# Gate matmuls on the residual stream, and 32-row matmuls padded to 128 rows, in a two-layer recurrent decoder step

## The chip, the cores and the metric

The kernel runs on one core of a Trainium2 chip. The metric is device time in microseconds (us): the median of three runs is 2811.98 us, from 2808.73 to 2813.22. The engines are named as in the profile: PE (TensorE matmuls), PEld (its weight loads), DVE (VectorE), ACT (ScalarE), POOL (GpSimd) and SP (SyncE). POOL computes little here. It mostly issues DMAs.

## The reference

A trunk of two layers runs over 256 prompt tokens and 8 samples of 4 tokens each, 288 columns in all. Layer 0 mixes with a diagonal state-space model and gated linear attention, layer 1 with an mLSTM of 4 heads. Each layer is followed by a squared-ReLU MLP. The change concerns layer 1, cut here to what matters:

```python
xn = rmsnorm(h, W['norm_mix'][layer])
proj = xn @ W['w_in_odd'][o]            # q, k, v, output gate, then 8 columns: ig, fg
ig = proj[..., 4*ML_WIDTH : 4*ML_WIDTH + ML_HEADS] + b_i
fg = proj[..., 4*ML_WIDTH + ML_HEADS :] + b_f
# per head: fcum, dmat, m come from ig and log_sigmoid(fg)
w  = exp(dmat - m[..., None])
sc = (q @ k.T) * w
num = sc @ v + wp[..., None] * (q @ cm)        # cm: 512 x 512 memory of the head
den = sum(sc, -1) + wp * (q @ nm)
h   = num / maximum(abs(den), exp(-m))[..., None]
c_new = decay * cm + sum_s wk * k_s v_s        # written out for all 8 samples
```

Every sample has its own 512 x 512 memory per head. All of these memories are read from HBM, updated and written back (64 pieces of 512 KB in and 64 out).

## The kernel before, in words

The residual stream lives in SBUF as `h` (tile `hr`), 16 blocks of 128 features by 288 columns, in f32. Every large product takes three matmuls in a reduced format: the weight is split into `wh` (ACT, L187) and `wl` (DVE, L188), the activation into `xh` and `xl`, where `xh` is `h` times the norm weight, rounded, and `xl` the rest. `mm` (L202 to L204) issues the three products per 128 x 128 block of weight. Weights come in pieces of 512 x 256 (`raw`, by SP). There are four buffers each of `raw`, `wh` and `wl`, and a cast waits until PE has finished with the buffer that it overwrites. So casts run one to two pieces ahead of PE, no more.

`run` goes through the list of pieces. After each it gives every side generator a turn (`pump`). So matmuls, casts and side work are interleaved in one fixed order per engine, settled when the program is built, and each engine works through its list strictly in that order. The side generators here are `ml_gates` (once, at the start of layer 1), `ml_head` (one per head), and `ml_mem`.

`ml_gates` multiplies the 8 gate columns of the weight (tile `wg`, zero-padded to 32 columns) with `xh` and then with `xl`: 32 plain f32 matmuls, four at a time on the four 32-column strips of the array (L1289). Its loads (L1272 to L1280) are on POOL.

`ml_head(h)` builds the weights `w`: 128 x 416 with the prompt's three blocks in columns 0 to 383 and the samples' block in columns 384 to 415, where only 32 partitions are used. DVE adds the masks (L1418 to L1420), ACT takes exponentials (L1421 to L1424), PE computes the scores (L1429), DVE multiplies (L1431, L1432). Later PE sums `w` for the denominators (L1482 to L1485) and multiplies it with the values `vt1` for the numerators (L1500 to L1502). The samples' parts, L1484 and L1502, contract over 32 partitions, all others over 128. L1484 runs once per head, L1502 four times. `w` has one buffer.

`ml_mem` walks through the 64 memory pieces. For each, PE makes an update, DVE applies it to the tile `cin` (L1563), POOL stores the tile (L1565), and then POOL loads the piece that is six ahead into the same buffer (L1533). That load waits until the store has landed. While it waits, POOL does nothing else.

Of the kernel before, what the change touches and what calls it, by code (L numbers as in the profile page):

```python
# [7 lines left out]
F32 = mybir.dt.float32  # L8
# [3 lines left out]
ALU = mybir.AluOpType  # L12
# [3 lines left out]
T = 288  # L16
TP = 256
NS = 32
D = 2048
ND = D // 128  # L20
# [1225 lines left out]
class Layer1:  # L1246
    def ml_open(self):
        self.mlc = ExitStack()
        pool = lambda n, b=1: self.mlc.enter_context(self.tc.tile_pool(name=n, bufs=b))
        p = self.mlp1 = pool("ml")  # L1250
        pool_d = self.mlc.enter_context(self.tc.tile_pool(name="mld", bufs=1, space=DRAM))
        self.q1 = p.tile([128, 4, T], F32, name="q1")
        self.k1 = p.tile([128, 4, T], F32, name="k1")
        self.vt1 = p.tile([128, 3, 512], F32, name="vt1")
        self.kw1 = p.tile([128, 3, 512], F32, name="kw1")
        self.hn, self.so, self.smp = {}, {}, {}
        self.yy = {}
        self.rb4 = p.tile([4, 608], F32, name="rb4")
        self.aT = p.tile([128, 3, 4], F32, name="aT")
        self.wkT = p.tile([128, 3, 4], F32, name="wkT")  # L1260
        self.dec = p.tile([128, 4], F32, name="dec")
        self.rb_dram = pool_d.tile([4, 608], F32, name="rb_dram")
        self.n0T = p.tile([128, 4, 32], F32, name="n0T")
        self.rbk = p.tile([128, T], F32, name="rbk")

    def ml_gates(self):
        nc, I, O = self.nc, self.I, self.O
        v, act = nc.vector, nc.scalar
        pc = self.tc.tile_pool(name="mlg", bufs=1, side="right")
        p = pc.__enter__()  # L1270
        wg = p.tile([128, ND, 32], F32, name="wg")
# [7 lines left out]
        n0 = p.tile([32, 512], F32, name="n0r")  # L1279
        nc.gpsimd.dma_start(out=n0, in_=I["state_mlstm_n"][0].rearrange("b h d -> (b h) d"))  # L1280
        yield
        yield
        v.tensor_scalar(out=self.rbk, in0=self.rbc, scalar1=512.0 ** -0.5, scalar2=None, op0=ALU.mult)
        ps = self.pss.tile([128, T], F32, name="s")
        for i in range(4):
            for x in (self.xh, self.xl):
                for c in range(4):
                    k = 4 * i + c
                    nc.tensor.matmul(ps[32 * c:32 * c + 32, :], lhsT=wg[:, k, :], rhs=x[:, k, :].bitcast(F32),  # L1289
                                     start=i == 0 and x is self.xh, stop=i == 3 and x is self.xl)  # L1290
        gs = p.tile([128, T], F32, name="gs")
        v.tensor_mul(out=gs, in0=ps, in1=self.rbc)
        yield
# [105 lines left out]
    def ml_head(self, h):  # L1399
        nc, I, O = self.nc, self.I, self.O  # L1400
        v, act = nc.vector, nc.scalar
        q, k, vt, kw = self.q1, self.k1, self.vt1, self.kw1
        yield from self.until("gates")
        p = self.mlh
# [10 lines left out]
        yield  # L1415

        w = p.tile([128, 416], F32, name="w")
        v.tensor_add(out=w[:, 0:128], in0=bb[:, 0:128], in1=self.c("tri"))  # L1418
        v.tensor_add(out=w[:, 256:384], in0=bb[:, 128:256], in1=self.c("tri"))
        v.tensor_add(out=w[0:32, 384:416], in0=bb[0:32, TP:T], in1=self.c("tri_s")[0:32])  # L1420
# [5 lines left out]
        ps = self.pss.tile([128, 416], F32, name="s")  # L1426
        for s0, n, t0, t1, o in ((0, 128, 0, 256, 0), (128, 128, 128, 256, 256), (256, 32, 256, 288, 384)):
            for d in range(4):
                nc.tensor.matmul(ps[0:n, o:o + t1 - t0], lhsT=k[:, d, s0:s0 + n], rhs=q[:, d, t0:t1],  # L1429
                                 start=d == 0, stop=d == 3)  # L1430
# [4 lines left out]
        for i, n in enumerate((128, 128, 32)):  # L1435
            ps = self.pss.tile([128, 4, 128], F32, name="s")
            for d in range(4):
# [9 lines left out]
                        op=ALU.mult)  # L1447
        qn = p.tile([128, 4, NS], F32, name="qn")
        v.tensor_tensor(out=qn.rearrange("p d (b s) -> p d b s", s=4), in0=qp.rearrange("p d (b s) -> p d b s", s=4),
                        in1=self.n0T[:, :, h:32:4].rearrange("p d (b o) -> p d b o", o=1).to_broadcast([128, 4, 8, 4]),  # L1450
                        op=ALU.mult)
# [10 lines left out]
        ps = self.pss.tile([128, 128], F32, name="s")  # L1462
        for i, (n, c) in enumerate(((128, "selp"), (128, "selp"), (32, "sels"))):
            for d in range(4):
                nc.tensor.matmul(ps[32 * d:32 * d + 32, :], lhsT=self.c(c)[0:n], rhs=kw[0:n, i, d * 128:d * 128 + 128],  # L1465
                                 start=i == 0, stop=i == 2)
# [13 lines left out]
        ps = self.pss.tile([128, T], F32, name="s")  # L1480
        on = self.ones
        nc.tensor.matmul(ps[:, 0:256], lhsT=on, rhs=w[:, 0:256], start=True, stop=False)  # L1482
        nc.tensor.matmul(ps[:, 128:256], lhsT=on, rhs=w[:, 256:384], start=False, stop=True)
        nc.tensor.matmul(ps[:, TP:T], lhsT=on[0:32], rhs=w[0:32, 384:416], start=True, stop=False)  # L1484
        nc.tensor.matmul(ps[:, TP:T], lhsT=on, rhs=qn[:, 0, :], start=False, stop=True)  # L1485
        rec = s["rec"] = p.tile([128, T], F32, name="rec", bufs=2)
        act.activation(out=rec, in_=ps, func=AF.Abs)
# [9 lines left out]
        for e in range(4):  # L1497
            es = slice(e * 128, e * 128 + 128)
            ps = self.pss.tile([128, T], F32, name="s")
            nc.tensor.matmul(ps[:, 0:256], lhsT=vt[:, 0, es], rhs=w[:, 0:256], start=True, stop=False)  # L1500
            nc.tensor.matmul(ps[:, 128:256], lhsT=vt[:, 1, es], rhs=w[:, 256:384], start=False, stop=True)  # L1501
            nc.tensor.matmul(ps[:, TP:T], lhsT=vt[0:32, 2, es], rhs=w[0:32, 384:416], start=True, stop=True)  # L1502
            v.tensor_mul(out=hn[:, e, :], in0=ps, in1=rec)
            yield

        for d in range(4):
            ds = slice(d * 128, d * 128 + 128)
            ps = self.pss.tile([128, 512], F32, name="s")
# [371 lines left out]
```

## Time and profile before

| what | value |
|---|---|
| runs, median (lowest to highest) | 2811.98 us (2808.73 to 2813.22) |
| profiled execution | 2810.88 us, span 2809.1 us |
| mean granted TensorE clock | 0.996 |
| PE busy | 2780.6 us (99%) |
| DVE, ACT, POOL busy | 62%, 48%, 8% |
| HBM traffic over the span | 181 GB/s |

PE has work in flight for nearly the whole span, and the chain of work that ended last is made of PE's pieces. The layer-1 mixer lies between about 1300 and 1910 us. There the DMA engines carry the memory pieces beside the weights: they are busy 67% to 82% of the time, against 55% in the MLP between 500 and 1300 us.

Times of single instructions in a timeline are start, duration, engine, line, what is written from what, and in brackets the idle time before it and what ended it. A plain f32 matmul shows as two records of PE.

### The profile page before, as it was taken

How to read it: one execution, taken by the hardware profiler on the slowest of the kernel's cores; microseconds unless marked ns; L12 is line 12 of the kernel's file. 1: busy time of each engine (PE TensorE's matmuls, PEld its weight loads, DVE VectorE, ACT ScalarE, POOL GpSimd, SP SyncE). 2: the span in 40 equal slices, each digit the busy share in tenths (PEclk: the TensorE clock that was granted, in tenths of full speed). 3: DMA queues.
4: the chain of work that ended last, by engine and by line, in shares of the span. 5: the costliest groups of instructions: out<-in, count | busy, mean ns of one | idle time of the engine just before them, and what ended most of it. 6: DMA issues, size and time to landing. Idle time of an engine off the chain costs nothing.

```text
span 2809.1 us, 52656 instructions
## 1 busy us (share of the span) xinstructions
PE 2780.6 (99%) x20680; PEld 2692.6 (96%) x20680; DVE 1728.4 (62%) x3259; ACT 1344.2 (48%) x2460; POOL 212.3 (8%) x326
## 2 busy tenths in 40 slices
PE   9999999999999999999999999999999999999999
PEld 8988999999999999999988898889999999999999
DVE  7887668555555555556566665867655555555555
ACT  5646755544444444445433343445544444444445
POOL 3110112000000000000112222210000000000000
PEclk9999999999999999999999999999999999999999
DMA  7454567555555555555677878875555555555554
GB/s 218 123 160 136 160 198 227 159 171 166 165 163 166 162 168 164 165 165 145 198 230 240 279 241 269 271 254 173 164 167 162 169 165 165 160 170 160 169 165 136
DMA packets 449656, 511.87 MB, mean 182 GB/s; under 512 B 23298, under 2 KB 423324, under 8 KB 449376
## 3 DMA queue, kind: packets, MB, share of 16 engines
q1 hardware_dynamic: 414320, 412.67, 48.7%
q0 software_dynamic: 28096, 90.16, 10.1%
q10 hardware_dynamic: 6992, 5.68, 0.6%
q8 instruction: 163, 2.67, 0.4%
q14 instruction: 85, 0.70, 0.1%
HBM read 460.08 MB, written 47.56 MB: 181 GB/s over the span
## 4 chain that ended last, share of the span: by engine, by line
PE 52%; ACT 0%; DVE 0%; issue 0%; DVEq 0%
PE g L202 16%; PE g L203 15%; PE g L204 15%; PE s L1561 1%; PE n L1555 1%; PE s L1510 1%; PE s L1429 0%; PE s L1500 0%; PE s L1438 0%; PE s L1502 0%; PE s L1465 0%; PE s L1501 0%; PE s L1587 0%; PE s L1382 0%; ACT wh L187 0%
## 5 line engine op out<-in xcount | busy, mean ns | idle before, releaser
L187 ACT ACTIVATE wh<-raw 128x512 fp32r<-128x512 f32 x1556 | 962.5, 629 | 1199.0 <-PE g L203 1151.7
L188 DVE TENSOR_TENSOR wl<-raw,wh 128x512 fp32r<-128x512 f32 x1556 | 1036.5, 689 | 662.8 <-ACT wh L187 651.0
L202 PE MATMUL g<-xh,wh 128*128 128x288 f32 x3856 | 1157.5, 300 | 3.0 <-DVE gy L948 1.4
L204 PE MATMUL g<-xh,wl 128*128 128x288 f32 x3856 | 1137.2, 295 | 3.4 <-DVE wl L188 3.4
L203 PE MATMUL g<-xl,wh 128*128 128x288 f32 x3856 | 1140.0, 296 | 0.0
L202 PEld LDWEIGHTS g<-xh,wh 128*128 128x128 f32 x3856 | 725.3, 188 | 14.4 <-issue 9.5
L204 PEld LDWEIGHTS g<-xh,wl 128*128 128x128 f32 x3856 | 728.0, 189 | 5.0 <-DVE wl L188 4.9
L203 PEld LDWEIGHTS g<-xl,wh 128*128 128x128 f32 x3856 | 726.3, 188 | 5.2 <-issue 3.3
L203 PE MATMUL g<-hl,wh 128*128 128x288 f32 x2048 | 606.2, 296 | 0.0
L204 PE MATMUL g<-hh,wl 128*128 128x288 f32 x2048 | 605.2, 296 | 0.0
L202 PE MATMUL g<-hh,wh 128*128 128x288 f32 x2048 | 604.7, 295 | 0.0
L202 PEld LDWEIGHTS g<-hh,wh 128*128 128x128 f32 x2048 | 389.1, 190 | 0.0
L204 PEld LDWEIGHTS g<-hh,wl 128*128 128x128 f32 x2048 | 384.0, 188 | 0.0
L203 PEld LDWEIGHTS g<-hl,wh 128*128 128x128 f32 x2048 | 383.7, 187 | 0.0
L1737 DVE TENSOR_TENSOR hr<-hr,g 128x288 f32<-128x288 f32 x256 | 116.4, 455 | 186.5 <-PE g L204 186.5
L1729 ACT ACTIVATE us<-sq 128x288 f32<-128x288 f32 x128 | 56.9, 445 | 146.3 <-DVE sq L1728 146.3
L1728 DVE SCALAR_TENSOR_TENSOR sq<-g,rbc 128x288 f32<-128x288 f32 x128 | 58.5, 458 | 94.5 <-PE g L204 94.3
L1563 DVE SCALAR_TENSOR_TENSOR cin<-cin,wps,s 128x512 f32<-128x512 f32 x128 | 89.7, 743 | 7.2 <-PE s L1561 6.5
L1533 POOL DMA_DIRECT2D cin<-in_state_mlstm_c_dram x64 | 45.3, 708 | 316.3 <-DMA out_sample_mlstm_c_dram<-cin 293.8
L1344 POOL DMA_DIRECT2D out_sample_mlstm_m_dram<-mo x1 | 0.6, 615 | 838.7 <-DVE mk L1348 838.7
L1730 ACT ACTIVATE hh<-us 128x288 fp32r<-128x288 f32 x128 | 57.0, 445 | 4.1
L203 PE MATMUL g<-yl,wh 128*128 128x288 f32 x192 | 56.7, 295 | 0.0
(506 smaller groups left out, 1939.7 us busy)
## 6 DMA issues: line engine op xcount, KB each, us to landing
raw<-in_w_mlp_up_dram SPq DMA_DIRECT2D x256, 512.0 KB, 3.7
raw<-in_w_mlp_down_dram SPq DMA_DIRECT2D x256, 512.0 KB, 3.7
raw<-in_w_in_odd_dram SPq DMA_DIRECT2D x128, 512.0 KB, 4.8
raw<-in_w_in_even_dram SPq DMA_DIRECT2D x64, 512.0 KB, 4.1
cin<-in_state_mlstm_c_dram POOLq DMA_DIRECT2D x64, 512.0 KB, 5.2
out_sample_mlstm_c_dram<-cin POOLq DMA_DIRECT2D x64, 512.0 KB, 5.7
raw<-in_w_out_even_dram SPq DMA_DIRECT2D x32, 512.0 KB, 4.6
raw<-in_w_out_odd_dram SPq DMA_DIRECT2D x32, 512.0 KB, 3.6
```

The source lines that it names most:

```text
L187: nc.scalar.activation(out=wh[:, 0:n], in_=src, func=AF.Copy)
L188: nc.vector.tensor_tensor(out=wl[:, 0:n], in0=src, in1=wh[:, 0:n].bitcast(F32), op=ALU.subtract)
L202: nc.tensor.matmul(g.ps[j], lhsT=wh, rhs=xh, start=opens and k == 0, stop=False)
L203: nc.tensor.matmul(g.ps[j], lhsT=wh, rhs=xl, start=False, stop=False)
L204: nc.tensor.matmul(g.ps[j], lhsT=wl, rhs=xh, start=False, stop=closes and k == n - 1)
L1510: nc.tensor.matmul(ps, lhsT=kw[:, i, ds], rhs=vt[:, i, :], start=i == 0, stop=i == 1)
L1533: nc.gpsimd.dma_start(out=cin[g], in_=part(I["state_mlstm_c"], g))
L1563: v.scalar_tensor_tensor(out=t[:, b, :], in0=t[:, b, :], scalar=wp[:, c:c + 1], in1=pb, op0=ALU.mult, op1=ALU.add)
L1728: nc.vector.scalar_tensor_tensor(out=t, in0=ps, scalar=0.0, in1=self.rbc, op0=ALU.max, op1=ALU.mult)
L1729: nc.scalar.activation(out=sq, in_=t, func=AF.Square)
L1730: nc.scalar.activation(out=hh[:, j, :], in_=sq, func=AF.Copy)
L1737: nc.vector.tensor_add(out=self.h[:, j, :], in0=self.h[:, j, :], in1=ps)
```

## The change

Three edits, with nothing moved between turns of the generators:

1. `ml_gates` multiplies `wg` by the norm weight on DVE as soon as its turn comes (one turn ahead of the matmuls), and the matmuls then read `h` instead of `xh` and `xl`: 16 matmuls instead of 32.
2. The samples' matmuls in denominators and numerators run over all 128 partitions. For that the 96 unused partitions must hold zeros: POOL clears the samples' columns of `w` in every head, over all 128 partitions, before DVE writes the first 32.
3. In the same way POOL clears the samples' third of `vt1`, once, when layer 1 is opened.

```diff
@@ ml_open
         self.vt1 = p.tile([128, 3, 512], F32, name="vt1")
+        self.nc.gpsimd.memset(self.vt1[:, 2, :], 0.0)
@@ ml_gates
         yield
+        v.tensor_tensor(out=wg[:, :, 0:8], in0=wg[:, :, 0:8], op=ALU.mult,
+                        in1=self.gmix[1].rearrange("p (k o) -> p k o", o=1).to_broadcast([128, ND, 8]))
         yield
         v.tensor_scalar(out=self.rbk, in0=self.rbc, scalar1=512.0 ** -0.5, scalar2=None, op0=ALU.mult)
         ps = self.pss.tile([128, T], F32, name="s")
         for i in range(4):
-            for x in (self.xh, self.xl):
-                for c in range(4):
-                    k = 4 * i + c
-                    nc.tensor.matmul(ps[32 * c:32 * c + 32, :], lhsT=wg[:, k, :], rhs=x[:, k, :].bitcast(F32),
-                                     start=i == 0 and x is self.xh, stop=i == 3 and x is self.xl)
+            for c in range(4):
+                k = 4 * i + c
+                nc.tensor.matmul(ps[32 * c:32 * c + 32, :], lhsT=wg[:, k, :], rhs=self.h[:, k, :], start=i == 0, stop=i == 3)
@@ ml_head
         w = p.tile([128, 416], F32, name="w")
+        nc.gpsimd.memset(w[:, 384:416], 0.0)
         v.tensor_add(out=w[:, 0:128], in0=bb[:, 0:128], in1=self.c("tri"))
         v.tensor_add(out=w[:, 256:384], in0=bb[:, 128:256], in1=self.c("tri"))
         v.tensor_add(out=w[0:32, 384:416], in0=bb[0:32, TP:T], in1=self.c("tri_s")[0:32])
...
-        nc.tensor.matmul(ps[:, TP:T], lhsT=on[0:32], rhs=w[0:32, 384:416], start=True, stop=False)
+        nc.tensor.matmul(ps[:, TP:T], lhsT=on, rhs=w[:, 384:416], start=True, stop=False)
...
-            nc.tensor.matmul(ps[:, TP:T], lhsT=vt[0:32, 2, es], rhs=w[0:32, 384:416], start=True, stop=True)
+            nc.tensor.matmul(ps[:, TP:T], lhsT=vt[:, 2, es], rhs=w[:, 384:416], start=True, stop=True)
```

In the changed kernel the lines up to L1254 keep their numbers. L1255 is the memset of `vt1`, L1283 the product of `wg`, L1419 the memset of `w`. The three mask additions are L1420 to L1422, the memory lines L1565 (DVE), L1567 (store) and L1535 (load).

What stands on POOL around the turn in which head 2 makes its `w`, before. The names with `cin` are memory pieces. In brackets stands what a row waits for: `DVE` is a count of DVE's work, `DMASW` one of POOL's own DMAs.

```order
L1565 DMA out_sample_mlstm_c_dram<-cin_18521 128x2x512 [waits DVE_49]
L1533 DMA cin_18951<-in_state_mlstm_c_dram 128x2x512 [waits DMASW4_49,DMASW3_49]
L1565 DMA out_sample_mlstm_c_dram<-cin_18604 128x2x512 [waits DVE_49]
L1533 DMA cin_18994<-in_state_mlstm_c_dram 128x2x512 [waits DMASW6_49,DMASW5_49]
L1565 DMA out_sample_mlstm_c_dram<-cin_18659 128x2x512 [waits DVE_49]
L1533 DMA cin_19104<-in_state_mlstm_c_dram 128x2x512 [waits DMASW7_49,DMASW0_49]
```

And in the changed kernel:

```order
L1567 DMA out_sample_mlstm_c_dram<-cin_18509 128x2x512 [waits DVE_49]
L1535 DMA cin_18939<-in_state_mlstm_c_dram 128x2x512 [waits DMASW4_49,DMASW3_49]
L1567 DMA out_sample_mlstm_c_dram<-cin_18592 128x2x512 [waits DVE_49]
L1535 DMA cin_18982<-in_state_mlstm_c_dram 128x2x512 [waits DMASW6_49,DMASW5_49]
L1419 MEMSET w_18986 128x32 [waits PE_49,Activation_49]
L1567 DMA out_sample_mlstm_c_dram<-cin_18647 128x2x512 [waits DVE_49]
L1535 DMA cin_19093<-in_state_mlstm_c_dram 128x2x512 [waits DMASW7_49,DMASW0_49]
```

The memset has come in behind a store and the load that waits for it. This is the 28th store of the 64. In head 1 it stands behind the 8th store and its load, in head 3 behind the 40th, and in head 0 ahead of the first load.

What stands on DVE at the same place, before. `cin_18604` is the tile of the 28th store, `wl` are casts, `us` the first piece of the values.

```order
L1563 SCALAR_TENSOR_TENSOR cin_18604<-cin_18604,wps_17696,s_18987 128x512 [waits DMASW5_49,DMASW4_49,PE_49]
L1563 SCALAR_TENSOR_TENSOR cin_18604<-cin_18604,wps_17696,s_18990 128x512 [waits PE_49]
L1538 TENSOR_TENSOR km_18996<-ks0_17704,cst_89 128x1024
L1418 TENSOR_TENSOR w_18998<-bc_18606,cst_89 128x128 [waits DMASW6_49]
L1419 TENSOR_TENSOR w_18998<-bc_18606,cst_89 128x128
L1420 TENSOR_TENSOR w_18998<-bc_18606,cst_89 32x32
L188 TENSOR_TENSOR wl_19033<-raw_18953,wh_19032 128x512 [waits DVE_49,DMAHW3_49,PE_49,Activation_49]
L188 TENSOR_TENSOR wl_19037<-raw_18953,wh_19036 128x512 [waits DVE_49,PE_49,Activation_49]
```

And in the changed kernel:

```order
L1565 SCALAR_TENSOR_TENSOR cin_18592<-cin_18592,wps_17684,s_18975 128x512 [waits DMASW5_49,DMASW4_49,PE_49]
L1565 SCALAR_TENSOR_TENSOR cin_18592<-cin_18592,wps_17684,s_18978 128x512 [waits PE_49]
L1540 TENSOR_TENSOR km_18984<-ks0_17692,cst_89 128x1024
L1420 TENSOR_TENSOR w_18986<-bc_18594,cst_89 128x128 [waits DMASW6_49]
L1421 TENSOR_TENSOR w_18986<-bc_18594,cst_89 128x128
L1422 TENSOR_TENSOR w_18986<-bc_18594,cst_89 32x32 [waits Pool_49]
L188 TENSOR_TENSOR wl_19022<-raw_18941,wh_19021 128x512 [waits DVE_49,DMAHW3_49,PE_49,Activation_49]
L188 TENSOR_TENSOR wl_19026<-raw_18941,wh_19025 128x512 [waits DVE_49,PE_49,Activation_49]
```

The rows are the same but for one wait: the third addition now waits for POOL, and all later casts stand behind it on DVE. The same wait is there in every head.

What stands on POOL where layer 1 is opened, before. The two stores are the last of layer 0, `bi` is a bias of the gates.

```order
L1137 DMA out_sample_gla_dram<-s0_5624 128x2x256 [waits DMASW3_49,DVE_49]
L1137 DMA out_sample_gla_dram<-s0_5718 128x2x256 [waits DMASW5_49,DVE_49]
L1272 MEMSET wg_15584 128x512 [waits DMASW1_49,DMASW6_49,DMASW0_49,DMASW7_49,PE_49,Pool_49]
L1273 DMA wg_15584<-in_w_in_odd_dram 128x16x8 [waits Pool_49]
L1275 DMA bi_15587<-in_mlstm_b_i_dram 4x1
```

And in the changed kernel:

```order
L1137 DMA out_sample_gla_dram<-s0_5624 128x2x256 [waits DMASW3_49,DVE_49]
L1137 DMA out_sample_gla_dram<-s0_5718 128x2x256 [waits DMASW5_49,DVE_49]
L1255 MEMSET vt1_15536 128x512 [waits DVE_49,PE_49,Activation_49]
L1273 MEMSET wg_15585 128x512 [waits DMASW6_49,DMASW1_49,DMASW7_49,DMASW0_49,Pool_49]
L1274 DMA wg_15585<-in_w_in_odd_dram 128x16x8 [waits Pool_49]
```

The loads of `ml_gates` follow the memset of `vt1`, which waits for PE, DVE and ACT; `vt1` takes over memory that the MLP ahead of it used.

## Rows read from the trace of the kernel before

**Rows 1.** Page, part 1: busy time, share of the span, instructions.
```profile
PE 2780.6 (99%) x20680; PEld 2692.6 (96%) x20680; DVE 1728.4 (62%) x3259; ACT 1344.2 (48%) x2460; POOL 212.3 (8%) x326
```
**Rows 2.** Timeline of PE, gate matmuls: first and last of eight groups.
```profile
1309.52 0.69 PE L1289 MATMUL s<-xh,wg 128*32 128x288 f32 x8
...
1312.94 0.67 PE L1289 MATMUL s<-xl,wg 128*32 128x288 f32 x8
```
**Rows 3.** Timeline of PE, one numerator of head 0, samples' part third.
```profile
1409.92 0.39 PE L1501 MATMUL s<-w,vt 128*128 128x128 f32 x2
1410.24 0.40 PE L1502 MATMUL s<-w,vt 32*128 32x32 f32 x2
1410.57 0.40 PE L202 MATMUL g<-xh,wh 128*128 128x288 f32 x1
```
**Rows 4.** Timeline of PE, four f32 matmuls of 32 columns over 128 partitions.
```profile
1905.16 0.97 PE L1587 MATMUL s<-cst,oi 128*128 128x32 f32 x8
1905.97 0.38 PE L202 MATMUL g<-yh,wh 128*128 128x288 f32 x1
```
**Rows 5.** One line's instructions, L1502: durations min/median/max in ns, records.
```profile
L1502 PE MATMUL s<-w,vt x32: 271/282/292, 1410.2 to 1834.3; 32*128 32x32 f32 x32
```
**Rows 6.** Timeline of POOL around head 2's w: 26th and 28th store, 28th load.
```profile
1617.26 0.72 POOL L1565 DMA_DIRECT2D out_sample_mlstm_c_dram<-cin  x1
...
1632.11 0.73 POOL L1565 DMA_DIRECT2D out_sample_mlstm_c_dram<-cin  x1
1637.40 0.70 POOL L1533 DMA_DIRECT2D cin<-in_state_mlstm_c_dram  x1 [4.55 <-DMA out_sample_mlstm_c_dram<-cin]
```
**Rows 7.** Timeline of DVE and ACT at the same place, head 2.
```profile
1617.47 1.40 DVE L1563 SCALAR_TENSOR_TENSOR cin<-cin,wps,s 128x512 f32<-128x512 f32 x2
...
1620.33 0.17 DVE L1420 TENSOR_TENSOR w<-bc,cst 32x32 f32<-32x32 f32 x1
1621.99 1.29 DVE L188 TENSOR_TENSOR wl<-raw,wh 128x512 fp32r<-128x512 f32 x2 [1.49 <-ACT wh L187]
...
1623.66 0.17 DVE L1432 TENSOR_TENSOR w<-w,s 32x32 f32<-32x32 f32 x1
...
1621.13 0.31 ACT L1424 ACTIVATE w<-w,aT 32x32 f32<-32x32 f32 x1
```
**Rows 8.** Timeline of PE, the transposes of k in heads 1, 2 and 3.
```profile
1482.09 0.60 PE L1438 MATMUL s<-cst,k 128*128 128x128 f32 x4
...
1627.81 0.60 PE L1438 MATMUL s<-cst,k 128*128 128x128 f32 x4
...
1738.88 0.60 PE L1438 MATMUL s<-cst,k 128*128 128x128 f32 x4
```
**Rows 9.** Timelines of DVE and POOL, heads 1 and 3: third addition, 8th and 40th load.
```profile
1472.60 0.17 DVE L1420 TENSOR_TENSOR w<-bc,cst 32x32 f32<-32x32 f32 x1
...
1483.19 0.70 POOL L1533 DMA_DIRECT2D cin<-in_state_mlstm_c_dram  x1 [6.16 <-DMA out_sample_mlstm_c_dram<-cin]
...
1731.39 0.17 DVE L1420 TENSOR_TENSOR w<-bc,cst 32x32 f32<-32x32 f32 x1
...
1739.56 0.70 POOL L1533 DMA_DIRECT2D cin<-in_state_mlstm_c_dram  x1 [5.44 <-DMA out_sample_mlstm_c_dram<-cin]
```
**Rows 10.** One line's instructions, L1565: all 64 stores, issue to landing.
```profile
DMA to landing us min/median/max: 3.5/5.7/8.7
```
**Rows 11.** Timeline of PE in layer 0, its longest wait.
```profile
279.04 0.70 PE L811 MATMUL n<-eh,hr 128*128 128x72 f32 x2 [2.98 <-ACT hr L792]
```
**Rows 12.** Busy time by stretch, PE alone: us, busy (records), granted clock, DMA share, GB/s.
```profile
284.20:288.40 4.20, 4.20 (x19) 0.50 0.00 0
500.00:1300.00 800.00, 800.00 (x6002) 1.00 0.55 165
```
**Rows 13.** Line L1273, the load of wg, and timelines of POOL and DVE.
```profile
487.69 1.18 POOL L1273 DMA_DIRECT2D wg<-in_w_in_odd_dram  x1 [0.29 <-POOL wg L1272]
...
DMA to landing us min/median/max: 5.5/5.5/5.5
...
1299.55 0.46 DVE L1737 TENSOR_TENSOR hr<-hr,g 128x288 f32<-128x288 f32 x1 [1.14 <-PE g L204]
...
1306.47 0.69 DVE L188 TENSOR_TENSOR wl<-raw,wh 128x512 fp32r<-128x512 f32 x1 [0.91 <-ACT wh L187]
```

## The prediction

> **What bounds the kernel now.** I read the page first: busy times and the chain of waits. PE has work in flight for 99% of the span [rows 1], and the chain that ended last runs through its matmuls. So each microsecond that PE saves comes off the time, and each that it waits goes on, as long as other engines keep up. Then I read PE's timeline at the three places that the diff touches, for what they cost. Then I read the order of the changed kernel for new waits, and the timelines of the engines at both ends of each new wait. The reader is to see two things. The matmul edits are worth some microseconds at a PE that never waits there. And three of the new memsets stand on POOL behind transfers on which POOL waits far longer than that.
>
> **The gate matmuls.** The 32 matmuls run in eight groups of 8 records. From the first group to the last are 3.42 us for seven steps, 0.489 us a group [rows 2]. Four groups go: 1.95 us off. They stand between other PE work, so all of it counts. The product on DVE covers 128 elements in each of 128 partitions. DVE has 0.91 us of idle time between two casts at this place [rows 13], so it costs nothing if `wg` is there.
>
> **Is `wg` there?** Its load moves. Before, it was issued at 487.69 and had 800 us to spare [rows 13]. Now it stands on POOL behind the memset of `vt1`, which waits for the MLP. The last sum of that MLP on DVE starts at 1299.55 [rows 13]. Two memsets of 0.5 us and a gap follow (my estimate from the distance of the old memset of `wg` to its load, 0.8 us), so the load goes out near 1300.9 and lands near 1306.4, at the 5.5 us it took before [rows 13]. DVE comes to the product after the cast that starts at 1306.47 and takes 0.69, at 1307.2. PE starts its gates at 1309.52 [rows 2]. With the slowest landing of the stores, 8.7 us [rows 10], it would land at 1309.6 and PE would wait half a microsecond. I take 0; up to 3 us is conceivable, as DVE's casts stand behind the product too.
>
> **The padded matmuls.** At one numerator the second record of L1501 starts 0.12 after the first (0.39 for two records that last 0.27 each by themselves), at 1410.04, and L1502 follows only 0.20 later; its second record starts at about 1410.36, and the next weight's product again 0.21 later [rows 3]. Where 32 columns are multiplied over 128 partitions, 8 records and the step to the next product take 0.81 us, 0.10 each [rows 4]. So both steps, into the 32-row matmul and out of it, cost 0.10 more than they would over 128 rows: 0.21 per place. L1502 stands for 32 records, 16 places [rows 5]; L1484 adds one per head, 4. Together 20 x 0.21 = 4.2 us off. If the extra steps came from something other than the rows it would be 0; more than 0.25 a place, 5 us, is not there to be saved.
>
> **The memset of `w`.** The memset itself is short. The point is where it stands. In head 2 it comes behind the 28th store and the load that waits for that store to land. That load is issued at 1637.40 and takes 0.70 [rows 6], so POOL would clear `w` at about 1638.2. DVE comes to the third addition at 1620.33 [rows 7]. The reason for the lag: DVE has the piece ready at 1618.87, but POOL is two stores behind, and stores it only at 1632.11 [rows 6, 7]. DVE would stand for nearly 18 us. Behind the addition are the next two casts, and ACT's next casts stand behind its exponential of the same block.
>
> PE goes on with the casts that it has. By the order of the changed kernel its first instruction that needs what is behind the stall is L1438, the transposes of k, which need a PSUM buffer that DVE frees. PE reaches them at 1627.81 [rows 8]. From the third addition until DVE has freed that buffer are 3.5 us in the trace (1620.33 to the end of L1432 at 1623.83), of which 0.6 is ACT still busy with earlier exponentials, from 1620.50 to 1621.13 [rows 7]; those will be done. So PE goes on 2.9 us after the memset: at 1641.2, after a wait of 13.4 us. This is the upper end: with the casts standing, no weights are loaded, and stores land faster. POOL needed 20.1 us from the 26th store to the 28th load, three turns of 6.7 [rows 6]. At the fastest landing of 3.5 us [rows 10] and 0.7 for the issue, a turn is 4.2; two turns of that are 5.0 us earlier, a wait of 8.4. I take 11.0, the middle.
>
> Heads 1 and 3 go the same way with one turn left instead of two. Head 1: load at 1483.19, memset done at 1484.1, PE on at 1487.0 against 1482.09, so 4.9 us [rows 8, 9]; with one turn 2.5 faster, 2.4. Head 3: load at 1739.56, PE on at 1743.4 against 1738.88, so 4.5; at the least 2.0 [rows 8, 9]. I take 4.0 for each, nearer to the upper ends, since the weights already ordered still run during the first part of the stall. In head 0 the memset stands ahead of the first load, and nobody waits. In sum 19.0 us, from 12.8 to 22.8.
>
> **The clock after the waits.** In layer 0 PE waits 2.98 us once [rows 11], and the products behind it run at half clock, 1.2 instead of 2.4 GHz: 19 records in 4.2 us, 0.221 each, against 0.133 in the MLP [rows 12]. That is 19 x 0.088 = 1.7 us lost in that stretch; from the end of the wait, 279.04, to 288.40 are 9.4 us, so at most 4.7. My waits are longer than this one. I take 2.0 each, near the dense stretch: 6.0 us, from 0 (no fall) to 14.
>
> The page TensorE: Matmul & The Clock Gate of the Trainium skill (Part 1: The HAM clock gate) says that the throttled state is the default and that only activity lifts it. By that rule each of the three waits ends in a slow stretch, as in the sum; if the row of layer 0 were a chance event, the sum would lack its 6.0.
>
> **Sum**, against the profiled execution's 2810.88: -1.95 - 4.2 + 19.0 + 6.0 = +18.85, so 2829.7. The median of the three runs lies 1.1 higher, and I say 2830. The ends of these terms give 2810.88 - 7.0 + 12.8 = 2816.7 and 2810.88 - 1.95 + 22.8 + 14 = 2845.7.
>
> **Rivals.**
>
> *Only the savings show* (the other side). POOL clears `w` when its turn comes in the program and not behind the waiting load, or the stores land before DVE comes. Place: L1419 in heads 1 to 3; price: nothing instead of 25 us; it decides if the memset is done within 4.6 us of DVE's arrival in every head (PE's slack in head 2, 1627.81 - 2.9 - 1620.33, and the same in head 3; 6.6 in head 1). Time 2810.88 - 6.15 = 2804.7. For it: a store can land in 3.5 us. Against it: 17 us in head 2 are five times that, and the order puts the memset behind the load. Chance 0.06. The page TensorE: Matmul & The Clock Gate of the Trainium skill (Part 1, on the engine queues) calls GpSimd's queue strict first in, first out; by that rule this rival has no way to come about in head 2, and the trace's lag of the 28th store agrees.
>
> *Short waits, no fall of the clock.* Stores land at their fastest, and the clock stays: 2810.88 - 6.15 + 12.8 = 2817.5. For it: all weight loads cease in the stall. Against it: the memory pieces' own loads still run beside the stores. Chance 0.15.
>
> *Long waits and a long slow stretch.* Waits as in the old timeline and three stretches like the whole of the one in layer 0: 2810.88 - 6.15 + 22.8 + 14 = 2841.5. Chance 0.12.
>
> *The padding saves nothing.* The extra steps around L1502 remain, as other matmuls on 32 columns remain in the same stretches: 2829.7 + 4.2 = 2833.9. Chance 0.08. *`wg` is late* as well, by up to 3 us: 2833. Chance 0.04.
>
> My forecast has 0.55. The range reaches from the short waits, 2817, to the long ones, 2841. What a measurement of this kernel can tell from no change is about 0.2%, 5.6 us: from 2806.4 to 2817.6. Faster than that is most of the first rival, 0.05. Within it are the rest of that rival and half of the short waits, 0.09. Slower is 0.86.
>
> **What would show it.** In the new profile POOL's memset of `w` starts right behind a load of `cin` in heads 1 to 3, and DVE's third addition has idle time before it that ends by POOL: near 18 us at most in head 2, 11 and 9 in the others. PE's waits before L1440 (the old L1438) are the longest of the trace, some 11 us in head 2 and 4 in heads 1 and 3, each with a granted clock near 0.5 behind it. The gates have four groups, and the steps around the samples' matmuls are 0.10. I am wrong if DVE's additions have no such idle time, if PE finds other work during it, or if the gates wait for `wg`.

## The result, and the profile after

The changed kernel takes 2826.35 us (median of 6 runs, 2821.84 to 2829.35) against 2809.83 us for the kernel before in the same comparison (median of 6 runs): a ratio of 1.0052, 95% interval 1.0042 to 1.0062. It is slower. Its profiled execution took 2821.84 us, span 2820.1, the shortest of the six, so its rows show the loss at its smallest. A second profile of the same kernel, told of among the experiments, took 2827.30, and both are read here. Two single runs of later experiments, 3818.72 us of the version that clears once and 8576.91 us of the one with POOL's memset in head 2 alone, lie far from all others; they count in the medians given there, but not in the ratios.

The page of the changed kernel, part 1, answers to [rows 1]:

```profile
PE 2778.1 (99%) x20648; PEld 2693.4 (96%) x20648; DVE 1727.4 (61%) x3260; ACT 1344.8 (48%) x2460; POOL 213.4 (8%) x331
```

PE is busy for 2.5 us less and the span is 11 us longer. The page alone shows no more than that: PE now waits somewhere.

The gates [rows 2], in the timeline of PE of the changed kernel (start, duration, what it did):

```profile
1309.51 2.15 PE L1291 MATMUL s<-hr,wg 128*32 128x288 f32 x32
1311.59 0.40 PE L202 MATMUL g<-xh,wh 128*128 128x288 f32 x1
```

Half of the records are gone, and the next weight follows at 1311.59. In the kernel before it stands at 1313.54:

```profile
1313.54 0.40 PE L202 MATMUL g<-xh,wh 128*128 128x288 f32 x1
```

Nothing waits at the start either, as POOL and DVE show around the load of `wg` [rows 13]:

```profile
1299.63 0.53 POOL L1255 MEMSET vt<- 128x512 f32 x1 [815.30 <-PE g L204]
1300.09 0.53 POOL L1273 MEMSET wg<- 128x512 f32 x1
1300.91 1.18 POOL L1274 DMA_DIRECT2D wg<-in_w_in_odd_dram  x1 [0.29 <-POOL wg L1273]
```

```profile
1306.47 0.69 DVE L188 TENSOR_TENSOR wl<-raw,wh 128x512 fp32r<-128x512 f32 x1 [0.91 <-ACT wh L187]
1307.08 0.28 DVE L1283 TENSOR_TENSOR wg<-wg,cols 128x128 f32<-128x128 f32 x1
```

The load goes out 813 us later than before, and still the product on DVE that needs it has no idle time in brackets.

One numerator of head 0 [rows 3], timeline of PE of the changed kernel:

```profile
1408.85 0.39 PE L1503 MATMUL s<-w,vt 128*128 128x128 f32 x2
1409.07 0.31 PE L1504 MATMUL s<-w,vt 128*128 128x32 f32 x2
1409.21 0.38 PE L202 MATMUL g<-xh,wh 128*128 128x288 f32 x1
...
1413.13 0.31 PE L1504 MATMUL s<-w,vt 128*128 128x32 f32 x2
```

From the start of the last prompt part (L1503) to the start of the next weight's product are 0.36 us; before it was 0.65 [rows 3]. Read start to start, from 1409.07 to 1413.13, numerators follow each other at 4.06.

Now the waits. The view of waits of DVE, and of PE, in the changed kernel (engine and line that wait, for whom: us in total, times, longest):

```profile
DVE w L1422 <- POOL w L1419: 28.6, 3, 13.6
```

```profile
PE s L1440 <- DVE w L1434: 9.1, 1, 9.1
PE s L1440 <- DVE cin L1565: 4.0, 2, 2.3
```

Neither pair exists in the kernel before: there the third addition and the transposes of k stand without idle time [rows 7, 8, 9]. The same instructions in the three heads, in the timelines of POOL, DVE and PE of the changed kernel, answer to [rows 6 to 9]:

```profile
1477.76 0.70 POOL L1535 DMA_DIRECT2D cin<-in_state_mlstm_c_dram  x1 [6.56 <-DMA out_sample_mlstm_c_dram<-cin]
1478.45 0.14 POOL L1419 MEMSET w<- 128x32 f32 x1
...
1619.59 0.70 POOL L1535 DMA_DIRECT2D cin<-in_state_mlstm_c_dram  x1 [6.15 <-DMA out_sample_mlstm_c_dram<-cin]
...
1626.00 0.72 POOL L1567 DMA_DIRECT2D out_sample_mlstm_c_dram<-cin  x1
1631.33 0.71 POOL L1535 DMA_DIRECT2D cin<-in_state_mlstm_c_dram  x1 [4.60 <-DMA out_sample_mlstm_c_dram<-cin]
1632.03 0.14 POOL L1419 MEMSET w<- 128x32 f32 x1
```

```profile
1478.63 0.18 DVE L1422 TENSOR_TENSOR w<-bc,cst 32x32 f32<-32x32 f32 x1 [8.14 <-POOL w L1419]
...
1632.20 0.18 DVE L1422 TENSOR_TENSOR w<-bc,cst 32x32 f32<-32x32 f32 x1 [13.64 <-POOL w L1419]
...
1746.36 0.18 DVE L1422 TENSOR_TENSOR w<-bc,cst 32x32 f32<-32x32 f32 x1 [6.78 <-POOL w L1419]
```

```profile
1481.72 0.65 PE L1440 MATMUL s<-cst,k 128*128 128x128 f32 x4 [1.67 <-DVE cin L1565]
...
1635.28 1.09 PE L1440 MATMUL s<-cst,k 128*128 128x128 f32 x4 [9.15 <-DVE w L1434]
...
1749.46 1.11 PE L1440 MATMUL s<-cst,k 128*128 128x128 f32 x4 [2.31 <-DVE cin L1565]
```

This is to be read from the bottom up. PE waits for DVE, DVE waits for a memset that takes 0.14 us, and the memset is late because POOL sits in front of a load whose buffer is still being stored. A bracket of 13.64 ahead of an addition of 0.18 is the mark of a wrong queue: the work that is waited for is tiny, and its place in the queue is everything. The transposes themselves take 1.09 and 1.11 instead of 0.60 in heads 2 and 3, because the clock has fallen. PE's stretches of 4 us show that (stretch, its length, busy (records), granted clock, DMA share, GB/s):

```profile
1480.00:1484.00 4.00, 2.33 (x19) 1.00 0.70 231
...
1632.00:1636.00 4.00, 0.72 (x4) 0.50 0.51 145
1636.00:1640.00 4.00, 4.00 (x18) 0.50 0.79 241
1640.00:1644.00 4.00, 3.88 (x28) 0.99 0.46 153
...
1748.00:1752.00 4.00, 2.54 (x11) 0.66 0.68 219
1752.00:1756.00 4.00, 3.88 (x27) 0.91 0.87 254
```

After 1.67 us of waiting in head 1 the clock stays at 2.4 GHz; after 9.15 and 2.31 it is at 1.2 GHz for some microseconds (0.50; a value between 0.50 and 1.00, as in head 3, mixes the two levels).

### The profile page after: what moved, and what is told of

Read it like the earlier page. It is cut to its first block, busy times and chain, and to the rows that moved or that the text cites. A ratio compares the mean times of both kernels' runs of the same rounds, so it can differ in the third digit from the quotient of the medians.

```text
span 2820.1 us, 52597 instructions
## 1 busy us (share of the span) xinstructions
PE 2778.1 (99%) x20648; PEld 2693.4 (96%) x20648; DVE 1727.4 (61%) x3260; ACT 1344.8 (48%) x2460; POOL 213.4 (8%) x331
## 4 chain that ended last, share of the span: by engine, by line
PE 88%; issue 4%; DMA 3%; DVE 3%; ACT 1%; POOL 1%; ACTq 0%; SPq 0%; DVEq 0%; POOLq 0%
PE g L202 27%; PE g L203 27%; PE g L204 27%; DMA out_sample_mlstm_c_dram<-cin 3%; DVE wl L188 1%; PE s L1563 1%; PE n L1557 1%; PE s L1512 1%; PE n L811 1%; POOL cin L1535 1%; PE s L674 0%; ACT wh L187 0%; DMA hr<-in_x_prompt_dram 0%; PE n L808 0%; DVE hr L755 0%
## 5 line engine op out<-in xcount | busy, mean ns | idle before, releaser
L1565 DVE SCALAR_TENSOR_TENSOR cin<-cin,wps,s 128x512 f32<-128x512 f32 x128 | 89.7, 742 | 6.9 <-PE s L1563 6.3
L1535 POOL DMA_DIRECT2D cin<-in_state_mlstm_c_dram x64 | 45.3, 708 | 289.4 <-DMA out_sample_mlstm_c_dram<-cin 264.2
L1255 POOL MEMSET vt<- 128x512 f32 x1 | 0.5, 527 | 815.3 <-PE g L204 815.3
```

The costliest lines, as they stand in the source:

```text
L1535: nc.gpsimd.dma_start(out=cin[g], in_=part(I["state_mlstm_c"], g))
L1565: v.scalar_tensor_tensor(out=t[:, b, :], in0=t[:, b, :], scalar=wp[:, c:c + 1], in1=pb, op0=ALU.mult, op1=ALU.add)
```

## The experiments

Ratios are to the kernel before, timed on the same chip. The first four ran on one chip, the next four on another, the last two on a third.

**The memset on DVE.** Diff against the changed kernel:

```diff
-        nc.gpsimd.memset(w[:, 384:416], 0.0)
+        v.memset(w[:, 384:416], 0.0)
```

> The changed kernel with one edit: DVE instead of POOL clears the samples' columns of w. Theory A (the loss comes from the memset's place on POOL, behind a store's landing): no DVE wait for POOL at the third addition, no wait of PE at the transposes of k, and the whole saving shows, 1.95 us from the gates and 20 x 0.32 = 6.4 us from the padded matmuls (the step from L1503 to the next weight fell from 0.65 to 0.36 us in the changed kernel's trace, and 0.03 behind it): about 2801.5 us against 2809.8 before, ratio 0.997. Theory B (the padded matmuls or the reads of h are themselves slower, or the casts of the stretch lose time in another way): it stays above 2815. Theory C (any clearing of w right ahead of its first use costs, on whichever engine, because DVE is late with its casts): between, 2806 or more.

Measured: 2804.14 us (9 runs, 2799.81 to 2806.39), ratio 0.9972, 0.9962 to 0.9981. Neither wait is left. The timeline of DVE in head 2:

```profile
1617.37 0.09 DVE L1419 MEMSET w<- 128x32 f32 x1
1617.54 0.29 DVE L1421 TENSOR_TENSOR w<-bc,cst 128x128 f32<-128x128 f32 x1
1617.74 0.17 DVE L1422 TENSOR_TENSOR w<-bc,cst 32x32 f32<-32x32 f32 x1
```

One word of the program is worth 2826.35 - 2804.14 = 22.2 us (of two comparisons, whose medians of the kernel before are 2.0 apart). Against the kernel before on its own chip it is 7.7 us faster, where theory A had 8.4; theory B falls, and so does C, since the memset on DVE takes 0.09 us and nobody waits for it. What makes the change slow is the queue in which the memset stands, not the memset.

**The memset early, on POOL.** Diff against the changed kernel (the uses of `w[..., 384:416]` read `ws`):

```diff
         n9 = p.tile([128, 128], F32, name="n9")
...
+        ws = p.tile([128, NS], F32, name="ws", bufs=2)
+        nc.gpsimd.memset(ws, 0.0)
...
-        w = p.tile([128, 416], F32, name="w")
-        nc.gpsimd.memset(w[:, 384:416], 0.0)
+        w = p.tile([128, 384], F32, name="w")
```

> POOL still clears the samples' block in every head, but in a tile of its own with two buffers, right behind the memset of n9, one store and load or more earlier in POOL's order. Theory A: DVE finds it cleared, no wait; the same time as with DVE clearing, 2801.5 us, ratio 0.997. If POOL as such were the trouble (a wait of DVE for POOL costs wherever it stands): near the changed kernel's 2826 or at least above 2812.

Measured: 2799.57 us (5 runs, 2799.33 to 2803.79), ratio 0.9958, 0.9945 to 0.997, and no such waits. POOL can do the memset too, if it comes to it in time. This edit also gives the block a tile of its own; the version that clears once, below, keeps it in `w`.

**The memset alone.** Diff against the kernel before; it clears `w`, and nothing is saved:

```diff
         w = p.tile([128, 416], F32, name="w")
+        nc.gpsimd.memset(w[:, 384:416], 0.0)
```

> The kernel before plus the memset of w on POOL alone; matmuls and gates as before, so nothing is saved. Theory A: the whole loss without the savings. The changed kernel's trace has 13.1 us of PE waits at the transposes of k, and some 3 to 5 us of half clock behind them: 2809.8 + 16 to 25 = 2826 to 2835, ratio 1.006 to 1.009. Theory B: nothing to see, 2810.

Measured: 2833.93 us (5 runs, 2829.47 to 2837.17), ratio 1.0077, 1.0063 to 1.0091. Its view of PE's waits:

```profile
PE s L1439 <- DVE w L1433: 8.7, 1, 8.7
PE s L1439 <- DVE cin L1564: 7.0, 2, 3.6
```

Four memsets of 0.14 us cost some 22 us, without any other edit, as theory A had it. In this profile the clock falls behind all three waits (0.66 from 1484 to 1488, 0.50 and 0.53 from 1636 to 1644, 0.57 from 1756 to 1760).

**The gates alone.** The kernel before with edit 1 of the change and nothing else (the diff of `ml_gates`).

> The kernel before with the gate edit alone (product of wg on DVE, 16 matmuls on h); no memsets of vt1 and w, samples' matmuls over 32 rows. Expected: 1.95 us less, 2807.9 us, ratio 0.9993, with the load of wg back at about 487 us. If a fall of the clock near 1328 us, seen in the changed kernel's trace and not in the one before, belongs to the gate edit: about 1.2 us of it are given back, ratio 0.9997.

Measured: 2807.94 us (11 runs, 2805.10 to 2810.92), ratio 0.9988, 0.9979 to 0.9997: faster by 0.8 to 5.9 us. That holds the 1.95, and can't say it more closely, or settle whether the 1.2 us are given back.

**The padding alone.** The kernel before with the 20 padded matmuls, `vt1` cleared once, and `w` cleared by DVE. Two of its lines, the rest cut:

```diff
+        v.memset(w[:, 384:416], 0.0)
...
-            nc.tensor.matmul(ps[:, TP:T], lhsT=vt[0:32, 2, es], rhs=w[0:32, 384:416], start=True, stop=True)
+            nc.tensor.matmul(ps[:, TP:T], lhsT=vt[:, 2, es], rhs=w[:, 384:416], start=True, stop=True)
```

> The kernel before with the padding alone: vt's third piece is cleared once, the samples' block of w is cleared on DVE in each head, and the 20 matmuls of the samples run over 128 partitions. The gate product is as before. Theory (each place saves 0.31 us, as the shift between the two traces showed): 20 x 0.31 = 6.2 us off, 4 short memsets on DVE cost nothing: 2809.8 - 6.2 = 2803.6, ratio 0.9978. Rival A (0.21 a place, as predicted from the rows of before): -4.2, ratio 0.9985. Rival B (the padding saves nothing in the time, the shift between traces was the clock): ratio 1.000.

Measured: 2805.18 us (11 runs, 2800.13 to 2809.00), ratio 0.998, 0.9971 to 0.9989: 3.1 to 8.2 us off. Rival B falls; between 4.2 and 6.2 the time does not decide, but the trace does. The numerators start 4.06 apart, as in the changed kernel (before it was 4.37, from the row of 1410.24 in [rows 3] to its next at 1414.61):

```profile
1407.55 0.31 PE L1504 MATMUL s<-w,vt 128*128 128x32 f32 x2
1411.61 0.31 PE L1504 MATMUL s<-w,vt 128*128 128x32 f32 x2
```

**Cleared once for all heads.** Diff against the changed kernel:

```diff
-        w = p.tile([128, 416], F32, name="w")
-        nc.gpsimd.memset(w[:, 384:416], 0.0)
+        w = self.w1
@@ where the pool of the heads opens
+            self.w1 = self.mlh.tile([128, 416], F32, name="w")
+            self.nc.gpsimd.memset(self.w1[:, 384:416], 0.0)
```

> The changed kernel with w allocated once for all heads and its samples' block cleared once, on POOL, when the pool of the heads opens; nothing of it is cleared again, since the additions rewrite only the first 32 partitions. Theory (the loss is the memset's place behind POOL's waiting loads, and the buffer's own reuse costs nothing): no wait of DVE for POOL, no wait of PE ahead of the transposes of k, time as with the early clearing, 2798 to 2804, ratio 0.995 to 0.998. Rival (the loss comes from the reuse of w, whose old reader must be done before the new writer): waits of DVE or POOL for PE at the additions appear, ratio above 0.999.

Measured: 2803.72 us (11 runs), ratio 0.9976, 0.9966 to 0.9985. No wait of DVE for POOL and none of PE ahead of the transposes of k. The rival falls: `w` is reused in every head just the same, and nobody waits for its old reader.

**The memset on POOL in head 2 alone.** Diff against the changed kernel:

```diff
-        nc.gpsimd.memset(w[:, 384:416], 0.0)
+        (nc.gpsimd if h == 2 else v).memset(w[:, 384:416], 0.0)
```

> The changed kernel with POOL's memset of w in head 2 alone; in heads 0, 1 and 3 DVE clears it. Theory (each wait has its own price, and head 2's is 9 us of waiting and 2 to 3 us of half clock): against the variant that clears all on DVE, 2804.1, +11 to +13: 2815 to 2817, ratio 1.001 to 1.003; one DVE wait for POOL of 12 to 18 us, and none in heads 1 and 3. Rival (the first wait of head 1 sets the state of POOL's queue for the rest, so that head 2 alone costs less, as POOL then comes nearer to its turn): wait of PE in head 2 under 5 us, ratio below 0.999.

Measured: 2817.14 us (11 runs), ratio 1.0023, 1.0014 to 1.0032: 13.0 us above the variant with all memsets on DVE, from another comparison. Its row of PE in head 2, and DVE's waits:

```profile
1637.31 1.08 PE L1440 MATMUL s<-cst,k 128*128 128x128 f32 x4 [13.53 <-DVE w L1434]
```

```profile
DVE w L1422 <- POOL w L1419: 18.0, 1, 18.0
```

Head 2 alone carries more than half of the loss; its wait does not need those of the other heads, and the rival falls. The wait itself is longer than the theory's 9 us, in a profile that is 1.8 us above the median.

**The changed kernel once more.**

> The changed kernel itself once more, for one more profile: do the waits and the falls of the clock come again at the same places? Theory (waits are set by the order of POOL's queue): DVE waits for POOL at the third addition in heads 1, 2 and 3, 5 to 20 us each, PE 12 to 20 us in sum ahead of the transposes of k; time 2820 to 2830. Rival (the waits hang on when a store lands and differ from run to run by more than their half): sum of PE's waits below 8 or above 20.

Measured: 2827.30 us in one run. Its timelines of POOL, DVE and PE:

```profile
1618.15 0.72 POOL L1567 DMA_DIRECT2D out_sample_mlstm_c_dram<-cin  x1
1625.26 0.70 POOL L1535 DMA_DIRECT2D cin<-in_state_mlstm_c_dram  x1 [6.38 <-DMA out_sample_mlstm_c_dram<-cin]
1625.96 0.72 POOL L1567 DMA_DIRECT2D out_sample_mlstm_c_dram<-cin  x1
1631.13 0.70 POOL L1535 DMA_DIRECT2D cin<-in_state_mlstm_c_dram  x1 [4.45 <-DMA out_sample_mlstm_c_dram<-cin]
1631.83 0.72 POOL L1567 DMA_DIRECT2D out_sample_mlstm_c_dram<-cin  x1
1637.09 0.70 POOL L1535 DMA_DIRECT2D cin<-in_state_mlstm_c_dram  x1 [4.54 <-DMA out_sample_mlstm_c_dram<-cin]
1637.78 0.14 POOL L1419 MEMSET w<- 128x32 f32 x1
```

```profile
1637.96 0.18 DVE L1422 TENSOR_TENSOR w<-bc,cst 32x32 f32<-32x32 f32 x1 [17.60 <-POOL w L1419]
```

```profile
1482.02 1.12 PE L1440 MATMUL s<-cst,k 128*128 128x128 f32 x4 [3.57 <-DVE cin L1565]
...
1641.03 1.09 PE L1440 MATMUL s<-cst,k 128*128 128x128 f32 x4 [13.11 <-DVE w L1434]
...
1754.90 1.12 PE L1440 MATMUL s<-cst,k 128*128 128x128 f32 x4 [2.05 <-DVE cin L1565]
```

The waits are at the same places, 18.7 us in sum, as the theory had it. Why the longest is longer than in the first profile is seen from the rows. DVE comes to the addition at 1637.96 - 17.60 = 1620.4, soon after a store; the load that ends this turn of POOL goes out at 1625.26, 4.9 us later, and two more turns of 5.9 follow. In the first profile DVE came at 1632.20 - 13.64 = 1618.6, 1.0 us ahead of the load of 1619.59, and again two turns followed. So the number of turns is the same, and what differs is how far POOL was in its turn when DVE came: 3.9 us, nearly all of the 4.0 between the two waits of PE. The order of the queue sets the number of turns, and not this part.

**The two best versions side by side.** The early clearing and the clearing once, unchanged, on one chip.

> The variant that clears the samples' block early, in a tile of its own, once more, beside the variant that clears it once. In the first pair of traces both needed the same time from the first numerator to the last (419.0 and 418.8 us), and the 4 us between them lay before the heads, in stretches of half clock. Theory (those stretches come and go from run to run and from chip to chip, so the lead is none of the edit): on one chip the two medians lie within 2 us, ratio 0.996 to 0.998. Rival (the early memset changes something before the heads): again 2800 and 0.9958, 3 to 5 us below the other.

> The variant that allocates w once and clears it once, again, as the partner of the early clearing on the same chip. Theory: within 2 us of it, 2800 to 2804, ratio 0.996 to 0.998. Rival: 3 to 5 us above it.

Measured: 2800.32 us (6 runs), ratio 0.9965, 0.9953 to 0.9977, and 2803.62 us (9 runs), ratio 0.9972, 0.9962 to 0.9981. The medians lie 3.3 us apart, which is the rival's size, but the intervals of the ratios overlap, so the times settle neither. PE's first 400 us in the early clearing, and then in the clearing once:

```profile
0.00:400.00 400.00, 383.01 (x2935) 0.98 0.58 164
```

```profile
0.00:400.00 400.00, 381.73 (x2906) 0.97 0.57 162
```

The lead is there, ahead of all that the edits touch: 29 records, at 0.133 each 3.9 us. It is not the early clearing's alone: the profile of the gates alone has it too, without that edit, and of the single runs of both pairs eight of eleven with the early clearing lie below 2801 us, but also two of the twenty with the clearing once. Why it comes so much oftener with the early clearing stays open. Both versions beat the kernel before and the changed one.

## Why the prediction was right, point by point

The forecast was 2830, from 2817 to 2841, and slower with 0.86. The time is 2826.35. The mechanism is the one forecast: with the memset on DVE the loss is gone, and with the memset alone it is there. That the number is so near is in part luck, as the terms below show: some were too small and others too large.

*Gates, -1.95.* The next weight starts at 1311.59; before it was at 1313.54, so 1.95 came off there. What the sum lacked is behind it. Some 15 us later PE has two short waits in the gates' scans, 0.5 and 1.1 us, the same in both kernels (before, a third of 0.2 followed). The clock kept its level before and falls now, somewhere between 1320 and 1336. PE in this stretch, first in the kernel before, then in the changed one:

```profile
1320.00:1336.00 16.00, 14.21 (x108) 1.00 0.51 115
```

```profile
1320.00:1336.00 16.00, 14.38 (x100) 0.89 0.46 98
```

8 records fewer, at 0.133 each, are 1.1 us given back. Of nine profiles with the shorter gates six show this fall, and three do not (both of the early clearing, and the gates alone); of three without the edit none does. In these three with the shorter gates the first of the two waits ends at 1322.9 to 1323.2 us, in the six at 1325.2 to 1327.2. In the kernels with all 32 gate matmuls it ends at 1325.5 to 1328.7 without a fall, so the time alone does not decide, and what does stays open.

*`wg` late, 0.* Right to a tenth: issue forecast for 1300.9, seen at 1300.91; product on DVE forecast for 1307.2, seen at 1307.08, without a wait.

*Padding, -4.2.* This term was mis-sized. A place saves 0.65 - 0.36 = 0.29, and a start-to-start step 4.37 - 4.06 = 0.31, so 20 places are 6.2 us. The bound in the prediction, that more than 0.25 a place "is not there to be saved", was wrong. It priced the steps into and out of the 32-row matmul at 0.10 each, with the two records of the matmul itself unchanged between them. Record by record the steps came out nearly as said: 0.11 instead of 0.20 into the samples' matmul, and 0.11 instead of 0.20 out of it. What was held to be unchanged was not. The two records of that matmul lay 0.13 apart before (0.40 for the pair, of which the second lasts 0.27 [rows 3, 5]). Now they are 0.03 apart (0.31, of which the second lasts 0.28), so 0.10 more is saved, and 0.03 in the products behind. Durations of L1504's records in the changed kernel, to set beside [rows 5]:

```profile
L1504 PE MATMUL s<-w,vt x32: 195/236/276, 1409.1 to 1845.3; 128*128 128x32 f32 x32
```

The page TensorEngine Tiling (Array Packing) of the Trainium skill (Key Properties) states that a change of tiling mode drains TensorE. It gives no price; the trace agrees with it by the 0.09 at each of the two steps, without showing what passes inside. The 0.10 between the two records of one matmul do not lie at such a change, and their cause stays open.

*The waits of PE, 19.0.* 13.1 in the first profile and 18.7 in the second. By head:

| head | forecast (range) | first profile | second profile |
|---|---|---|---|
| 1 | 4.0 (2.4 to 4.9) | 1.67 | 3.57 |
| 2 | 11.0 (8.4 to 13.4) | 9.15 | 13.11 |
| 3 | 4.0 (2.0 to 4.5) | 2.31 | 2.05 |

In head 2 both profiles lie within the two bounds, one near each end. The bounds had counted POOL's turns at 4.2 and 6.7; they were 5.7 to 6.0, shorter than before, as had been thought possible once the casts stand. What the prediction left out is where in its turn POOL is when DVE comes. In heads 1 and 3 three of the four values lie near or under the lower ends, so the step that chose 4.0 there, "nearer to the upper ends", was the weaker one. In the version with head 2 alone its wait is 13.53, just above the upper end. The idle time of DVE was forecast as near 18 us at most, 11 and 9; it was 17.6, 10.0 and 6.5 in the second profile, and 13.6, 8.1 and 6.8 in the first. The slack that the prediction gave PE between DVE's arrival and its own need, 6.6 us in head 1 and 4.6 in heads 2 and 3, came out: DVE's idle time less PE's wait is 6.5, 4.5 and 4.5 in both profiles. So the chain from DVE to PE was right, and what was off is when POOL came to the memset.

*The clock, 6.0.* What a head lost beyond its wait is read from the stretch between the last numerator of one head and the first of the next, against the version that clears once (98.18, 128.14 and 136.54 us):

| into head | first profile | loss - wait | second profile | loss - wait |
|---|---|---|---|---|
| 1 | 100.06 | 1.88 - 1.67 = 0.2 | 103.43 | 5.25 - 3.57 = 1.7 |
| 2 | 139.63 | 11.49 - 9.15 = 2.3 | 143.55 | 15.41 - 13.11 = 2.3 |
| 3 | 140.57 | 4.03 - 2.31 = 1.7 | 140.38 | 3.84 - 2.05 = 1.8 |

4.3 and 5.8 us, close to three times 2.0. In head 2 of the first profile PE works at half clock from 1635.28 to about 1640, so half of 4.7 us is lost, 2.4; that accounts for the difference there. A wait of 13 us costs little more in clock than one of 2. The page TensorE: Matmul & The Clock Gate of the Trainium skill (Part 1: The HAM clock gate) calls the throttled state the default, which activity releases. The traces agree in that PE goes on at half clock after each of the waits from 2.05 us on and is back at full clock some microseconds later; after the wait of 1.67 it did not fall, so this sentence alone does not say which wait brings a fall.

*The sum.* With the measured terms the first profile gives -1.95 + 1.1 - 6.2 + 13.1 + 4.3 = +10.4 on 2810.88, so 2821.2, against 2821.84. The second gives -1.95 + 1.1 - 6.2 + 18.7 + 5.8 = +17.5, so 2828.3, against 2827.30. The forecast of 2829.7 was 7.9 us above the first profile, mostly by the waits (5.9), then by the padding (2.0) and the clock (1.7), with the 1.1 given back at the gates against them. It was 2.4 above the second, where waits and clock came out within 0.5 and the padding's 2.0 is the main part. The order of the queue, from which the prediction worked, does not say which of the two a run will be near to.

*The rivals.* Only the savings: forecast 2804.7 if POOL's place did not matter, and that is near what the memset on DVE gives, 2804.14, but not what the change gives: in heads 1 to 3 its memset starts 0.7 us after the load ahead of it was issued, never earlier. Short waits with no fall of the clock: the waits of the first profile are as short as that rival's 12.8 (13.1), but the clock fell in two heads of three. Long waits and a long slow stretch: no; where PE's wait was longest in the first profile, it goes on at 1635.28 and is at full clock again from about 1640, under 5 us later, where that rival had 9.4. Padding that saves nothing and a late `wg`: no.

## What to carry to other kernels

Before a small operation is given to an engine because that engine is idle, look at what stands ahead of it in that engine's queue: POOL was busy for 8% of the span, and a memset of 0.14 us behind one of its waiting loads cost PE 9 to 13 us of waiting. Clear a buffer's unused part where the buffer is made, once, or on the engine that writes it next. A small f32 matmul over few rows between matmuls over all rows is worth padding, if the zeros cost nothing: 0.31 us a place here.

## What the runs showed of the hardware

The same short waits do and do not bring the clock down. A wait of 1.67 us in head 1 left it at full, one of 2.05 in head 3 halved it. The two waits of 0.5 and 1.1 us at the gates left it at full in six profiles and brought it down in six others, all of these with the shorter gates ahead of them; what decides is not shown. The stretches of half clock in layer 0, which no edit touches, also differ from profile to profile, by 29 records or 3.9 us. One run therefore does not tell a saving of 2 us from them. What does tell it is the distance between two rows of one trace: the 0.31 us a place, and PE's slack of 4.5 us in head 2, came out the same in every profile read for them.
